# Moving the forget logits into the second half of the values, the spatial weights to another place and other banks, and a layer norm without its centring pass

## The chip, the cores and the metric

The kernel runs on one core of a Trainium2 chip. A core has five engines with queues of their own: TensorE (PE, matrix products into PSUM; PEld is its loading of weights), VectorE (DVE), ScalarE (ACT), GpSimd (POOL), and SyncE (SP), which here only issues DMAs. PSUM has eight banks of 128 x 512 floats. The metric is the device time of one execution in microseconds; the time of a kernel is the median of its runs.

## The reference

One layer of a streaming encoder over 512 positions of width 1024, in float32. What matters for the change is the first projection and the gated branch behind it:

```python
h = rmsnorm(x, norm_mix_g[i])
z = jnp.einsum('bsd,dc->bsc', h, w_in[i])
uv = jax.nn.gelu(z[..., :o1])
z_u, z_v = uv[..., :GMLP_WIDTH], uv[..., GMLP_WIDTH:]
...
v = z[..., o1 + 2 * FOX_WIDTH:o2]
f_logit = z[..., o2:o3]
...
# spatial gating: blocks of 128 positions, 8 groups of 128 channels
v = layernorm(z_v, ln_g, ln_b)
w = jnp.where(mask[None], w_s, jnp.zeros_like(w_s))
mixed = jnp.einsum('gts,bnsgc->bntgc', w, v) + b_s.T[None, None, :, :, None]
return z_u * mixed.reshape(B, S, GMLP_WIDTH)
```

The 16 forget logits of each position go through a log-sigmoid and a running sum over positions, which is added to the attention's scores. Behind the two branches stand the gates, the output projection, a gated MLP with a causal convolution (width 2816), an embedding add and a last RMSNorm.

## The kernel before

Every float32 product is made of three products of a split: a matrix is cut into a high part (a copy rounded to the fast type, on ScalarE, L144, L250 or L366) and a low part (the difference, on VectorE, L145, L251 or L367), and TensorE multiplies low by high, high by low and high by high. One such matmul has 128 x 128 stationary and 512 moving columns. Weights come in 512 KB pieces through a ring of raw buffers ("raw", three, and "more", five) into a ring of five split pairs ("whi", "wlo").

TensorE's order is written out by hand: the blocks with `tc.manual_schedule(engines={ET.PE})` keep the order of the program there. The orders of the other engines are set by a planner when the kernel is built, which simulates the engines and places an instruction when its inputs are due; each engine then works through its fixed order and waits in place.

The stages in question, in TensorE's order:

1. The first half of the values (512 columns, weight rows as moving operand, L227 to L231), woven with the transposes of the normalised input.
2. The forget logits (L554 to L591). Their weights (64 columns, of which 16 count) land in a part of tile S4l, are copied to S2l (L561) and their low part is taken (L562). Sixteen matmuls with 64 output columns (L568) write one bank; then come a chain on ScalarE and VectorE (L571 to L588) and a store to `cum_d`.
3. The second half of the values (`proj_N` with `rb_outer=False`, L612): four weight pairs, and for each the four row blocks, into four banks; 96 matmuls (L153 to L155), with `evac_v` at the end.
4. A gate projection (`gate_steps`, L167 to L171).
5. Two Strassen-like products (`wino_jobs`), for the gelu inputs of v and then of u: seven products P1, P7, P6, P2, P5, P4, P3 of 24 matmuls each, so 336 steps in all. They use as stationary operands the input itself and four sums of its quarters, split in tiles S1 to S4 (sums of L607): S3 serves P7, S2 P6, S1 P5 and S4 P3. Their results stand in banks "sc" (P1 and P2), "pt" (P7 and P4) and "pt", "av" (P6, P5, P3).
6. Inside the second of them stand the layer norm of v (L688 to L703, in tile zv) and the spatial weights: step 168 and 24 more, layer norm, 120 more, the transpose of the bias `bsr` (L708), 12 more, four transposes (L714), 6 more, four transposes, 6 more.
7. Another gate, then eight spatial mixes (`mix`, L719 to L737) woven with gates, and then attention, which reads `cum_d`.

The banks go by tags: "mm" has two, "sc" two, "pt" three, "av" one; an unnamed bank takes the next tag of `BANK_TURN`. The squares of the layer norm, the bias and weight transposes and the gates all use "mm".

Of the kernel before, what the change touches and what calls it, by code (L numbers as in the profile page):

```python
# [9 lines left out]
F32 = mybir.dt.float32  # L10
F32R = mybir.dt.float32r
AF = mybir.ActivationFunctionType
ALU = mybir.AluOpType
PSUM = bass.MemoryType.PSUM

P = 128
S = 512
D = 1024
NB = S // P
NK = D // P  # L20
# [9 lines left out]
N_FIRST = 1  # L30
# [13 lines left out]
def hybrid_block(  # L44
# [6 lines left out]
    nc = tc.nc  # L51
    V, A, G, T = nc.vector, nc.scalar, nc.gpsimd, nc.tensor
# [6 lines left out]
    w_in_v, w_a_v, w_b_v = kview(w_in[0]), kview(w_a[0]), kview(w_b[0])  # L59
# [10 lines left out]
    state = {"n": 0, "bank": 0, "ring": None, "more": None, "raw": 0, "pool": {}, "psum": None}  # L70
# [15 lines left out]
    def bank(tag=None):  # L86
        pool, bufs = state["psum"]
        if tag is None:
            tag = BANK_TURN[state["bank"] % len(BANK_TURN)]
            state["bank"] += 1  # L90
        return pool.tile([P, 512], F32, tag=tag, name=uid("bank"), bufs=bufs[tag])
# [38 lines left out]
    def more_tile():  # L130
        return state["more"].tile([P, D], F32, tag="more", name=uid("more"), bufs=X_BUFS)
# [52 lines left out]
    def load_N(wv, k0, nk, ch, subs=(None, None), between=None):  # L184
        res = []
        for j in range(nk // 2):
            k = k0 + 2 * j
            res.append(load_w(wv[:, k:k + 2, 512 * ch:512 * ch + 512], 2, 512, subs[j % 2]))
            if between:
                between(j)  # L190
        return res

    def proj_N(wv, k0, nk, act, ch, evac, rb_outer=True, subs=None):

        ahi, alo = act
        subs = subs or load_N(wv, k0, nk, ch)

        def part(bk, rb, j):
            r = ds(rb * P, P)
            for kk in range(2):  # L200
                k = 2 * j + kk
                mm3(bk, ahi[:, k, r], alo[:, k, r], subs[j][0][:, kk, :], subs[j][1][:, kk, :],
                    start=(k == 0), stop=(k == nk - 1))
        if rb_outer:
            for rb in range(NB):
                bk = bank()
                for j in range(nk // 2):
                    part(bk, rb, j)
                evac(bk, rb, ch)
        else:  # L210
            bks = [bank() for _ in range(NB)]
            for j in range(nk // 2):
                for rb in range(NB):
                    part(bks[rb], rb, j)
                    if j == nk // 2 - 1:
                        evac(bks[rb], rb, ch)

    def proj_N_steps(wv, k0, nk, act, ch, evac, subs=None):

# [16 lines left out]
    def steps(g, n):  # L236
        for _ in range(n):
            next(g)
# [118 lines left out]
    ident = consts.tile([P, P], F32, tag="ident", name="ident")  # L357
# [102 lines left out]
    def quarter(tag, dt=F32R):  # L460

        return ph.tile([P, D], dt, tag=tag, name=uid(tag))
# [97 lines left out]
    nc.sync.dma_start(wf_raw, w_in_v[:, :, 5120:5184])  # L560
    V.tensor_copy(wf2, wf_raw)  # L561
    V.tensor_tensor(wf2[:, :, 32:48], wf_raw[:, :, 0:16], wf2[:, :, 0:16].bitcast(F32), ALU.subtract)  # L562
    state["bank"] = 3
    bk = bank()
    with tc.manual_schedule(engines={ET.PE}):
        for k in range(8):
            for t in (1, 0):
                T.matmul(bk[0:64, :], wf2[:, k, :], hT[t][:, k, :],  # L568
                         start=(k == 0 and t == 1), stop=(k == 7 and t == 0))
    fz, fa, fb = fm[0][0:16, 0:512], fm[0][0:16, 512:], fm[1][0:16, 0:512]  # L570
    A.copy(fa, bk[32:48, :])  # L571
    V.scalar_tensor_tensor(fz, bk[0:16, :], bft[0:16, :], fa, ALU.add, ALU.add)
# [35 lines left out]
        split_out(sums[(0, 2, 1, 3)[n]], dst, full)  # L608

    state["bank"] = 0  # L610
    with tc.manual_schedule(engines={ET.PE}):
        proj_N(w_in_v[:, :, 4096:5120], 0, NK, hT, 1, evac_v, rb_outer=False)  # L612

    zv = zv_tile().rearrange("p (b c) -> p b c", b=NB)
# [15 lines left out]
    def gate_weights(n):  # L632
        return load_w(w_in_v[:, :, gate_col(n):gate_col(n) + P], 8, P)
# [37 lines left out]
    with tc.manual_schedule(engines={ET.PE}):  # L671
        run(gate_steps(0, "mm", gate_tile, None, G))
        units = wino_steps(wino_jobs(w_in_v, 1024, hT, sums, wino_rows(zv, gelu_zv))
                           + wino_jobs(w_in_v, 0, hT, sums, wino_rows(zu, gelu_zu)))
        steps(units, 168)
        gb = [more_tile(), more_tile()]
        nc.sync.dma_start(gb[0], rows_bc(ln_g[0], D))
        nc.sync.dma_start(gb[1], rows_bc(ln_b[0], D))

        wst = more_tile().rearrange("p (g s) -> p g s", g=8)  # L680
        nc.sync.dma_start(wst, w_s[0].rearrange("g t s -> t g s"))
        G.memset(wst[0:64, :, 64:128], 0.0)
        bsr = ph.tile([P, P], F32, tag="bsr", name="bsr")
        G.memset(bsr, 0.0)
        nc.sync.dma_start(bsr[0:8, :], b_s[0])
        steps(units, 24)

        nm, va = tiny("nm", NB), tiny("va", NB)  # L688
        V.tensor_tensor(nm, zs[:, 0:NB], zs[:, NB:], ALU.add)
        V.tensor_scalar(nm, nm, -1.0 / D, None, ALU.mult)  # L690
        sq = tiny("sq", 2 * NB, 1)
        for rb in range(NB):
            A.activation(zv[:, rb, :], zv[:, rb, :], AF.Identity, bias=nm[:, rb:rb + 1])
            for h in range(2):
                A.activation(bank("mm"), zv[:, rb, 512 * h:512 * h + 512], AF.Square,
                             accum_out=sq[:, NB * h + rb:NB * h + rb + 1])
        V.tensor_tensor(va, sq[:, 0:NB], sq[:, NB:], ALU.add)
        V.tensor_scalar(va, va, 1.0 / D, EPS, ALU.mult, ALU.add)
        y = rsqrt_of(va, NB)
        for rb in range(NB):  # L700
            V.scalar_tensor_tensor(zv[:, rb, :], zv[:, rb, :], y[:, rb:rb + 1], gb[0],
                                   ALU.mult, ALU.mult)
            V.tensor_tensor(zv[:, rb, :], zv[:, rb, :], gb[1], ALU.add)  # L703
        steps(units, 120)

        wsT = [quarter(f"S1{t}").rearrange("p (g t) -> p g t", g=8) for t in "hl"]
        bk = bank("mm")
        T.transpose(bk[:, 0:P], bsr, ident)  # L708
        V.tensor_copy(bsT, bk[:, 0:NK])
        steps(units, 12)  # L710
        for g0 in (0, 4):
            bk = bank("mm")
            for g in range(4):
                T.transpose(bk[:, g * P:(g + 1) * P], wst[:, g0 + g, :], ident)  # L714
            split_out(wsT, bk.rearrange("p (g t) -> p g t", g=4),
                      (slice(None), slice(g0, g0 + 4), slice(None)))
            steps(units, 6)

        def mix(g):  # L719
            c = slice(g * P, g * P + P)  # L720
            vp = quarter(f"S2{'hl'[g % 2]}").rearrange("p (t b c) -> p t b c", t=2, b=NB)
            vh, vl = vp[:, 0], vp[:, 1]
            split_out((vh, vl), zv[:, :, c], (slice(None),) * 3)
            bk = bank("sc")
            mm3(bk, wsT[0][:, g, :], wsT[1][:, g, :], vh, vl, True, True)
            an = quarter(f"S3{'hl'[g % 2]}", F32)[:, 0:512].rearrange("p (b c) -> p b c", b=NB)
            V.scalar_tensor_tensor(an, bk.rearrange("p (b c) -> p b c", b=NB), bsT[:, g:g + 1],
                                   zu[:, :, c], ALU.add, ALU.mult)
            yield
            bk = bank("pt")  # L730
            for n in range(NB):
                T.transpose(bk[:, n * P:(n + 1) * P], an[:, n, :], ident)
            ap = quarter(f"S4{'hl'[g % 2]}").rearrange("p (t r) -> p t r", t=2)
            split_out((ap[:, 0], ap[:, 1]), bk, (slice(None),) * 2)
            for t in range(2):
                G.dma_start(aT_d[t][g * P:g * P + P, :], ap[:, t].bitcast(F32))
            yield  # L737


        first, ahead, w_qk = N_FIRST, [gate_weights(N_FIRST)], []  # L740

        def mix_gates():
            for n in range(first, GATES[0] - 1):
                w = ahead.pop()
                if n + 1 < GATES[0] - 1:
                    ahead.append(gate_weights(n + 1))
                else:

                    w_qk.extend(qk_weights(pr) for pr in range(2))
                yield from gate_steps(n, "mm", gate_tile, w, G)  # L750

        run(units)
        fill = mix_gates()
        steps(fill, 24 * N_COVER)
        ms = [mix(g) for g in range(NK)]
        items = [ms[0], ms[1]]
        for g in range(2, NK):
            items += [ms[g - 2], ms[g]]
        items += [ms[NK - 2], ms[NK - 1]]
        weave(items, fill, 24 * N_MIX)  # L760
        run(fill)
# [234 lines left out]
    bk = bank()  # L996
# [249 lines left out]
```

## Time and profile before

| | us |
|---|---|
| median of 3 runs | 965.3 |
| lowest, highest | 964.53, 966.54 |
| the profiled execution | 964.26 |
| its span, first to last instruction | 962.5 |
| DVE busy | 596.9 |
| ACT busy | 465.6 |
| POOL busy | 118.4 |

The profile shows one execution. A row of a timeline has the start and the duration in us from the span's start, the engine, the line of the kernel, the operation, the tiles written and read, the shape and the count; in brackets stand the idle time of the engine before the row and what ended it. A matmul's displayed duration overlaps with the next one's start, since matmuls are pipelined. "PEclk" is the share of TensorE's full clock that was granted. The mean granted clock of the whole execution is 0.994.

### The profile page before, as it was taken

To read this page: it belongs to the slowest core of one execution; us is meant where nothing else is said; L and a number is where in the kernel's file an instruction comes from. 1 tells how busy PE (TensorE), PEld (TensorE's weight loads), DVE (VectorE), ACT (ScalarE), POOL (GpSimd) and SP (SyncE) were. 2 spreads that over 40 slices of the span, in tenths; PEclk is the share of its full clock that TensorE was granted. 3 is DMA by queue.
4 is the path that set the end of the run, shared out by engine and by line. 5 is a ranking of instruction groups with operands and counts; after the bars stand their busy time and mean duration, and the time that the engine had idled before them with its cause. 6 is when DMAs were issued, how large, how long until landed. Compare 5 with 4: busy or idle time off the path is not lost.

```text
span 962.5 us, 11722 instructions
## 1 busy us (share of the span) xinstructions
PE 936.6 (97%) x4375; PEld 774.9 (81%) x4375; DVE 596.9 (62%) x1025; ACT 465.6 (48%) x779; POOL 118.4 (12%) x116
## 2 busy tenths in 40 slices
PE   8899998999999998999999999999999999999995
PEld 6678886888888887888888888888888888888885
DVE  6866789657777888425644665664356553365754
ACT  7644685466666666424433554443143441244443
POOL 3000000343333201001000400000000000001225
PEclk9999999999999999999999999999999999999998
DMA  9512344753333331199841422224323323223202
GB/s 343 179 59 74 113 142 110 240 164 99 99 99 99 99 99 65 56 328 359 299 157 63 153 88 88 88 88 132 108 73 104 110 88 109 66 88 131 70 18 88
DMA packets 100292, 121.21 MB, mean 126 GB/s; under 512 B 5252, under 2 KB 70972, under 8 KB 100236
## 3 DMA queue, kind: packets, MB, share of 16 engines
q1 hardware_dynamic: 97740, 112.57, 36.1%
q0 software_dynamic: 2352, 7.64, 2.1%
q8 instruction: 34, 0.56, 0.2%
q10 hardware_dynamic: 144, 0.26, 0.1%
q14 instruction: 22, 0.18, 0.1%
HBM read 106.79 MB, written 13.66 MB: 125 GB/s over the span
## 4 chain that ended last, share of the span: by engine, by line
PE 88%; DVE 6%; ACT 2%; issue 1%; DMA 1%; POOL 1%; SPq 0%; POOLq 0%; DVEq 0%
PE bank L167 17%; PE bank L169 17%; PE bank L171 17%; PE bank L153 5%; PE bank L155 5%; PE bank L154 5%; PE bank L227 3%; PE bank L229 3%; PE bank L231 3%; PE bank L306 2%; PE bank L303 2%; PE bank L299 2%; PE bank L861 2%; PE bank L852 1%; PE bank L403 1%
## 5 line engine op out<-in xcount | busy, mean ns | idle before, releaser
L167 PE MATMUL bank<-slot,wlo 128*128 128x512 f32 (+1 forms) x744 | 295.0, 398 | 0.8 <-DVE S1l L367 0.8
L169 PE MATMUL bank<-slot,whi 128*128 128x512 f32 (+1 forms) x744 | 289.0, 389 | 0.0
L171 PE MATMUL bank<-slot,whi 128*128 128x512 f32 (+1 forms) x744 | 288.7, 389 | 0.0
L144 ACT CAST whi<-raw 128x1024 fp32r<-128x1024 f32 x130 | 136.0, 1047 | 137.9 <-PE bank L155 80.1
L145 DVE TENSOR_TENSOR wlo<-raw,whi 128x1024 fp32r<-128x1024 f32 x108 | 132.6, 1229 | 109.2 <-ACT whi L144 108.8
L171 PEld LDWEIGHTS bank<-slot,whi 128*128 128x128 f32 x744 | 139.7, 188 | 29.0
L167 PEld LDWEIGHTS bank<-slot,wlo 128*128 128x128 f32 x744 | 139.9, 188 | 25.0 <-DVE S1l L367 1.3
L169 PEld LDWEIGHTS bank<-slot,whi 128*128 128x128 f32 x744 | 140.2, 188 | 22.5 <-DVE slot L367 0.2
L145 POOL TENSOR_TENSOR wlo<-raw,whi 128x1024 fp32r<-128x1024 f32 x22 | 53.8, 2449 | 518.7 <-ACT whi L144 511.1
L153 PE MATMUL bank<-whi,slot 128*128 128x512 f32 (+1 forms) x232 | 88.6, 382 | 0.0
L155 PE MATMUL bank<-whi,slot 128*128 128x512 f32 (+1 forms) x232 | 88.6, 382 | 0.0
L154 PE MATMUL bank<-wlo,slot 128*128 128x512 f32 (+1 forms) x232 | 88.6, 382 | 0.0
L227 PE MATMUL bank<-whi,slot 128*128 128x512 f32 x152 | 59.9, 395 | 2.6 <-DVE slot L367 2.6
L231 PE MATMUL bank<-whi,slot 128*128 128x512 f32 x152 | 59.6, 392 | 0.0
L229 PE MATMUL bank<-wlo,slot 128*128 128x512 f32 x152 | 59.1, 390 | 0.0
L155 PEld LDWEIGHTS bank<-whi,slot 128*128 128x128 f32 x232 | 43.6, 188 | 8.5
L153 PEld LDWEIGHTS bank<-whi,slot 128*128 128x128 f32 x232 | 43.6, 188 | 8.5
L154 PEld LDWEIGHTS bank<-wlo,slot 128*128 128x128 f32 x232 | 43.6, 188 | 8.4
L1086 DVE SCALAR_TENSOR_TENSOR ul<-bank,cvT,ul 128x511 f32<-128x511 f32 x22 | 16.5, 750 | 50.9 <-ACT ul L1085 50.9
L834 ACT ACTIVATE t<-t,mn 128x512 f32<-128x512 f32 (+1 forms) x64 | 35.9, 562 | 10.4 <-DVE mn L831 7.5
L366 ACT CAST pth<-bank 128x512 fp32r<-128x512 f32 (+1 forms) x64 | 26.3, 428 | 24.8 <-PE bank L852 24.7
L227 PEld LDWEIGHTS bank<-whi,slot 128*128 128x128 f32 x152 | 28.6, 188 | 8.9 <-DVE slot L367 3.4
(278 smaller groups left out, 1357.1 us busy)
## 6 DMA issues: line engine op xcount, KB each, us to landing
raw<-in_w_up_dram SPq DMA_DIRECT2D x44, 512.0 KB, 3.5
raw<-in_w_in_dram SPq DMA_DIRECT2D x36, 512.0 KB, 4.5
raw<-in_w_down_dram SPq DMA_DIRECT2D x22, 512.0 KB, 3.2
more<-in_w_in_dram SPq DMA_DIRECT2D x20, 512.0 KB, 5.3
cum<-cum_d SPq DMA_DIRECT2D x8, 512.0 KB, 4.0
raw<-in_w_branch_b_dram SPq DMA_DIRECT2D x8, 512.0 KB, 3.6
slot<-aT_d SPq DMA_DIRECT2D x4, 1024.0 KB, 12.3
sg<-gate_d SPq DMA_DIRECT2D x16, 256.0 KB, 5.3
```

Source lines behind the costliest of these rows:

```text
L144: A.copy(hi, raw)
L145: (sub or V).tensor_tensor(lo, raw, hi.bitcast(F32), ALU.subtract)
L153: T.matmul(out_ap, alo, bhi, start=start, stop=False)
L154: T.matmul(out_ap, ahi, blo, start=False, stop=False)
L155: T.matmul(out_ap, ahi, bhi, start=False, stop=stop)
L167: T.matmul(out_ap, wl, ah, start=(n == 0 and k == 0), stop=False)
L169: T.matmul(out_ap, wh, al, start=False, stop=False)
L171: T.matmul(out_ap, wh, ah, start=False, stop=end)
L227: T.matmul(bk, alo[:, k, r], wh, start=(k == 0), stop=False)
L229: T.matmul(bk, ahi[:, k, r], wl, start=False, stop=False)
L231: T.matmul(bk, ahi[:, k, r], wh, start=False, stop=(k == nk - 1))
L834: A.activation(t, t, AF.Exp, scale=-1.0, bias=m, accum_out=rs[:, i:i + 1])
```

## The change

It has three parts. The forget logits' sixteen matmuls go from before the second half of the values to behind its first weight pair (24 matmuls), with a hook `after` in `proj_N`; the weights of the values are loaded ahead of them, and the bank counter is set so that the four value banks come first. The spatial weights are loaded into the quarter S3h, at 24 steps behind the layer norm, in place of a "more" buffer; bias and weights are transposed at steps 270, 295 and 301 in "sc" banks, the bias is copied by ScalarE in place of VectorE, and the load of the next gate's weights is issued before the weight transposes. The layer norm no longer centres v in a pass of its own on ScalarE: the squares take the negative mean as a bias, VectorE computes (v - mean) x gain before the variance is known, and then x 1/deviation + offset, where it computed v x 1/deviation x gain and + offset before.

```diff
-    def proj_N(wv, k0, nk, act, ch, evac, rb_outer=True, subs=None):
+    def proj_N(wv, k0, nk, act, ch, evac, rb_outer=True, subs=None, after=None):
...
                     if j == nk // 2 - 1:
                         evac(bks[rb], rb, ch)
+                if after:
+                    after(j)
...
-    state["bank"] = 3
-    bk = bank()
-    with tc.manual_schedule(engines={ET.PE}):
+    state["bank"] = 0
+    subs_v1 = load_N(w_in_v[:, :, 4096:5120], 0, NK, 1)
+    bk_f = []
+
+    def forget(j):
+        if j:
+            return
+        bk_f.append(bank())
         for k in range(8):
             for t in (1, 0):
-                T.matmul(bk[0:64, :], wf2[:, k, :], hT[t][:, k, :],
+                T.matmul(bk_f[0][0:64, :], wf2[:, k, :], hT[t][:, k, :],
                          start=(k == 0 and t == 1), stop=(k == 7 and t == 0))
+
+    with tc.manual_schedule(engines={ET.PE}):
+        proj_N(w_in_v[:, :, 4096:5120], 0, NK, hT, 1, evac_v, rb_outer=False, subs=subs_v1,
+               after=forget)
+    bk = bk_f[0]
...
     state["bank"] = 0
-    with tc.manual_schedule(engines={ET.PE}):
-        proj_N(w_in_v[:, :, 4096:5120], 0, NK, hT, 1, evac_v, rb_outer=False)
...
-        wst = more_tile().rearrange("p (g s) -> p g s", g=8)
-        nc.sync.dma_start(wst, w_s[0].rearrange("g t s -> t g s"))
-        G.memset(wst[0:64, :, 64:128], 0.0)
...
         for rb in range(NB):
-            A.activation(zv[:, rb, :], zv[:, rb, :], AF.Identity, bias=nm[:, rb:rb + 1])
             for h in range(2):
                 A.activation(bank("mm"), zv[:, rb, 512 * h:512 * h + 512], AF.Square,
-                             accum_out=sq[:, NB * h + rb:NB * h + rb + 1])
+                             bias=nm[:, rb:rb + 1], accum_out=sq[:, NB * h + rb:NB * h + rb + 1])
+            V.scalar_tensor_tensor(zv[:, rb, :], zv[:, rb, :], nm[:, rb:rb + 1], gb[0],
+                                   ALU.add, ALU.mult)
...
         for rb in range(NB):
-            V.scalar_tensor_tensor(zv[:, rb, :], zv[:, rb, :], y[:, rb:rb + 1], gb[0],
-                                   ALU.mult, ALU.mult)
-            V.tensor_tensor(zv[:, rb, :], zv[:, rb, :], gb[1], ALU.add)
-        steps(units, 120)
+            V.scalar_tensor_tensor(zv[:, rb, :], zv[:, rb, :], y[:, rb:rb + 1], gb[1],
+                                   ALU.mult, ALU.add)
+        steps(units, 24)
+
+        wst = quarter("S3h", F32).rearrange("p (g s) -> p g s", g=8)
+        nc.sync.dma_start(wst, w_s[0].rearrange("g t s -> t g s"))
+        G.memset(wst[0:64, :, 64:128], 0.0)
+        steps(units, 54)
+        bk = bank("sc")
+        T.transpose(bk[:, 0:P], bsr, ident)
+        A.copy(bsT, bk[:, 0:NK])
+        steps(units, 19)
+
+        first, ahead, w_qk = N_FIRST, [gate_weights(N_FIRST)], []
 
         wsT = [quarter(f"S1{t}").rearrange("p (g t) -> p g t", g=8) for t in "hl"]
-        bk = bank("mm")
-        T.transpose(bk[:, 0:P], bsr, ident)
-        V.tensor_copy(bsT, bk[:, 0:NK])
-        steps(units, 12)
         for g0 in (0, 4):
-            bk = bank("mm")
+            steps(units, 6)
+            bk = bank("sc")
             for g in range(4):
                 T.transpose(bk[:, g * P:(g + 1) * P], wst[:, g0 + g, :], ident)
             split_out(wsT, bk.rearrange("p (g t) -> p g t", g=4),
                       (slice(None), slice(g0, g0 + 4), slice(None)))
-            steps(units, 6)
...
-        first, ahead, w_qk = N_FIRST, [gate_weights(N_FIRST)], []
```

## The prediction

> **What bounds the kernel now.** First the head of the page and its chain that ended last.
>
> ```profile
> span 962.5 us, 11722 instructions
> PE 936.6 (97%) x4375; PEld 774.9 (81%) x4375; DVE 596.9 (62%) x1025; ACT 465.6 (48%) x779; POOL 118.4 (12%) x116
> PE 88%; DVE 6%; ACT 2%; issue 1%; DMA 1%; POOL 1%; SPq 0%; POOLq 0%; DVEq 0%
> ```
>
> TensorE is busy 97% of the span and is 88% of the chain. The change adds and removes no matmul, so only TensorE's gaps and its clock can give time: 962.5 - 936.6 = 25.9 us of gaps. The second view, the waits of TensorE, says which gaps belong to the edited code.
>
> ```profile
> PE bank L568 <- DVE S2l L562: 3.5, 1, 3.5
> PE bank L852 <- DVE ptl L367: 3.2, 3, 1.7
> PE bank L714 <- DVE bsT L709: 2.0, 1, 2.0
> PE bank L167 <- DVE S1l L367: 0.8, 1, 0.8
> ```
>
> The columns after the colon are total, times and longest. Three of these waits lie in the edited stretch: the forget logits (L568) for their split weights, the transposes of the spatial weights (L714) for a copy out of their bank, and the next gate projection (L167) for the bank after that. L852 is in attention, which the change does not touch. Third, the windows around these waits (columns: span, then busy time with count for PE, PEld, DVE, ACT, POOL, then PEclk, DMA share, GB/s).
>
> ```profile
> 46.20:49.00 2.80, 2.80 (x8) 1.54 (x9) 2.80 (x4) 0.00 (x0) 0.00 (x0) 0.61 0.66 192
> 49.00:51.50 2.50, 2.50 (x10) 1.42 (x9) 2.25 (x2) 0.00 (x0) 0.00 (x0) 0.75 0.89 283
> 51.50:154.30 102.80, 102.80 (x456) 84.71 (x454) 78.50 (x94) 59.95 (x88) 1.83 (x3) 1.00 0.32 95
> 124.00:144.00 20.00, 20.00 (x90) 16.54 (x89) 16.45 (x28) 16.88 (x29) 0.52 (x1) 1.00 0.57 165
> 144.00:154.00 10.00, 10.00 (x48) 8.13 (x46) 9.90 (x14) 3.86 (x5) 0.00 (x0) 1.00 0.60 156
> 154.00:164.00 10.00, 7.13 (x33) 5.38 (x32) 10.00 (x14) 6.89 (x10) 0.00 (x0) 1.00 0.35 94
> 159.20:206.00 46.80, 46.79 (x221) 38.67 (x222) 28.80 (x39) 22.60 (x36) 17.79 (x27) 1.00 0.59 192
> ```
>
> Two things are to be seen. After the first gap the granted clock is 0.61 and 0.75 for 5.3 us, so this wait is paid twice. And around the second and third gaps VectorE is full (9.90 of 10, then 10.00 of 10): TensorE waits for work that is small but stands in VectorE's queue. Between and behind the gaps TensorE has no idle time that could be had.
>
> **Part 1: the forget logits go behind the first quarter of the second value half.** The rows of TensorE's order in time (start, duration, line):
>
> ```profile
> 42.23 0.39 PE L231 MATMUL bank<-whi,slot 128*128 128x512 f32 x1
> 46.16 5.47 PE L568 MATMUL bank<-slot,S2l 128*64 128x512 f32 x16 [3.54 <-DVE S2l L562]
> 51.47 0.40 PE L153 MATMUL bank<-whi,slot 128*128 128x512 f32 x1
> ...
> 73.25 0.39 PE L167 MATMUL bank<-slot,wlo 128*128 128x512 f32 x1
> ```
>
> The second value half is 4 weight pairs x 4 row blocks x 6 = 96 matmuls from 51.47 to 73.25: 21.78 / 96 = 0.2269 us from start to start. The displayed 0.39 overlaps with the next one, so I count starts. The first half's last matmul should be followed at 42.23 + 0.23 = 42.46. The forget block starts at 46.16, 3.70 later, and its 16 matmuls take until 51.47, 5.31 us, where 16 x 0.2269 = 3.63 would do at full clock; 64 output columns in place of 128 should not make one longer, and the windows give the clock as the reason. So the place costs 3.70 + 1.68 = **5.38 us**.
>
> Afterwards the values run on at 42.46 if their first weights are split, 24 matmuls cover until 42.46 + 5.45 = 47.91, and then the forget block needs S2l. VectorE's rows:
>
> ```profile
> 41.28 1.22 DVE L145 TENSOR_TENSOR wlo<-more,whi 128x1024 fp32r<-128x1024 f32 x1
> ...
> 45.82 0.28 DVE L562 TENSOR_TENSOR S2l<-S4l,S2l 128x128 fp32r<-128x128 f32 x1
> ...
> 50.03 1.22 DVE L272 TENSOR_TENSOR raw<-more,raw 128x1024 f32<-128x1024 f32 x1
> ```
>
> The first split is done at 42.50, and only the second matmul (at 42.69) reads it: no wait. S2l is done at 46.10, 1.8 us before 47.91. So nothing is left of the stall, and the cover is those 24 matmuls; without them the price is the 3.70 again. Of the moved instructions, the value loads and splits now precede the Strassen sums (L607) in program order, which can only bring them forward in VectorE's queue; the loads on SP have landed by then, as the splits show. The chain behind the logits (log-sigmoid, scan, the store of cum_d) starts when the block ends, 47.91 + 3.63 = 51.54 against 51.47, so it stays put while TensorE moves 5.4 us ahead; its buffers are next read by the third Strassen product, over 30 us later. Cost nothing.
>
> **Part 2: the spatial weights and the bias.** The rows that price it:
>
> ```profile
> 138.53 0.39 PE L299 MATMUL bank<-whi,S1l 128*128 128x512 f32 x1
> ...
> 149.42 0.27 PE L708 MATMUL bank<-ident,bsr 128*128 128x128 f32 x1
> ...
> 153.90 0.40 PE L306 MATMUL bank<-whi,S4h 128*128 128x512 f32 x1
> 156.35 0.66 PE L714 MATMUL bank<-ident,more 128*128 128x128 f32 x4 [2.05 <-DVE bsT L709]
> ...
> 157.99 0.40 PE L306 MATMUL bank<-whi,S4h 128*128 128x512 f32 x1
> 159.21 0.50 PE L167 MATMUL bank<-slot,wlo 128*128 128x512 f32 x1 [0.83 <-DVE S1l L367]
> ...
> 164.83 0.39 PE L153 MATMUL bank<-S2h,S1l 128*128 128x512 f32 x1
> ```
>
> From start to start the stalls are 156.35 - 153.90 - 0.23 = 2.22 and 159.21 - 157.99 - 0.23 = 0.99, together **3.21 us**. The bias transpose moves from step 312 of the 336 (149.42) to step 270, 42 x 0.2269 earlier, at about 139.9; the weights' from 324 and 330 to 295 and 301, about 145.6 and 146.9 (all on the clock of the run before). They use the "sc" banks, which product P2 leaves at 138.53 as the row of P5 shows, so the gate behind them finds its "mm" bank unused and its 0.99 has no cause left. The copy to bsT now goes to ScalarE, which has 124-144 full at 16.88 of 20 but loses 4.3 us there (below), then 3.86 of 10.
>
> What must be ready is wst at step 295. It goes into S3h, dead once P7 is through:
>
> ```profile
> 127.10 0.34 SPq L677 DMA_DIRECT2D more<-in_gmlp_ln_g_dram  x1
> 132.50 0.34 SPq L678 DMA_DIRECT2D more<-in_gmlp_ln_b_dram  x1
> 134.19 0.38 SPq L681 DMA_DIRECT2D more<-in_gmlp_w_s_dram  x1
> ...
> 138.77 0.52 POOL L682 MEMSET more<- 64x512 f32 x1 [58.40 <-issue]
> ```
>
> P7 ends two products of 24 steps before P5 starts at 138.53, so S3h is free at 127.64 and asks for no later issue than 134.19; the clearing on POOL, which waits for the landing, ends at 139.29, 6.3 us before 145.6. On SP the load stands behind the two of the layer norm as before, and the next gate's weights are merely issued earlier, into a buffer that wst no longer takes. Nothing.
>
> **Part 3: layer norm without the centring pass.** By group (last numbers: busy, mean ns):
>
> ```profile
> L695 ACT ACTIVATE bank<-zv 128x512 f32<-128x512 f32 x8 | 4.7, 585 | 0.0
> L693 ACT ACTIVATE zv<-zv,nm 128x1024 f32<-128x1024 f32 x4 | 4.3, 1141 | 0.7 <-DVE nm L690 0.7
> L701 DVE SCALAR_TENSOR_TENSOR zv<-zv,qy,more 128x1024 f32<-128x1024 f32 x4 | 4.9, 1281 | 0.0
> L703 DVE TENSOR_TENSOR zv<-zv,more 128x1024 f32<-128x1024 f32 x4 | 4.8, 1215 | 0.0
> 206.91 0.72 ACT L834 ACTIVATE t<-t,mn 128x512 f32<-128x512 f32 x1
> ```
>
> ScalarE loses 4.3 us. A square with a per-row bias is not in the trace; it lies between the plain one, 0.585, and the exponential with a bias, 0.72, so at most 8 x 0.135 = 1.1 us come back; I take half. It is off TensorE's path. [...] VectorE keeps eight wide passes, four of them 0.07 longer each (+0.26), and loses the 0.15 of L709. But four of the eight move from behind the variance to before it, where VectorE had 20 - 16.45 = 3.55 us free.
>
> **Sum.** 5.38 + 3.21 = 8.59 us. Against the profiled execution's 964.26 (its span 962.5 and 1.76 around it) that gives 955.67; the median of the runs shown is 965.3, 1.04 above the profiled one, so the forecast is **956.7 us**.
>
> **The rivals.** *VectorE's backlog only moves (959.2).* TensorE would reach the first spatial mix (L153, 164.83) 3.21 us earlier against VectorE, at 161.62, and that needs the split of the values:
>
> ```profile
> 132.95 1.21 DVE L251 TENSOR_TENSOR wlo<-more,whi 128x1024 fp32r<-128x1024 f32 x1
> ...
> 163.14 0.68 DVE L367 TENSOR_TENSOR S2h<-zv,S2h 128x512 fp32r<-128x512 f32 x1
> ```
>
> It ended at 163.82. With the same order of work and none of the free 3.55 us used, TensorE waits 163.82 + 0.26 - 161.62 = 2.5 us there; if 2.5 of the 3.55 are filled, nothing. I take nothing, since the last layer norm pass comes before the gates' weight splits that now stand between, so those can step behind. Against it: the gain row is issued only at 127.10, and part of the free time lies before its landing.
>
> *The forget block waits in its new place (962.0).* VectorE is full until about 51.3 (last row of part 1). If L562 is ordered behind all of that, TensorE stands from 47.91 to 51.5 and the clock drops again, so nearly all of the 5.38 is lost and only part 2 remains: 965.3 - 3.2 = 962.1. One wide pass more ahead of it costs nothing, two some 0.5.
>
> *The slow clock is luck (958.4).* If a gap of 3.70 us slows the clock in some executions only, 1.68 of the sum is not there: 965.3 - 6.91. [...] Against it, the other runs (964.53 to 966.54) are none of them 1.68 below the profiled 964.26.
>
> *Slower: VectorE's queue is blocked by the layer norm (968).* The first passes now need the gain row at once, and it was issued at 127.10 and lands some 3.7 us after, the other row after 132.50. Were the order fixed so that both sets of four stand ahead of the Strassen splits, 4.9 us each plus a wait for a landing, the split at 132.95 with its product at 138.53 (4.4 us of slack to its end) is late by about 3 us, the later ones by up to 5, and the mix by the 2.5 above; with another slow clock (1.7) that is 12 us, more than the 8.6 gained. It decides from the point at which over 4.4 us are put ahead of that split.
>
> **How the numbers follow.** Forecast 0.70 (own range 954.5 to 958.0: the spread of the runs and half a us in attention's waits either way), backlog 0.12, forget late 0.07, clock luck 0.05, slower 0.06. The range 954.3 to 961.0 takes in the forecast, the backlog and the clock, and leaves out the forget block's worst and the slower case, some 0.15 with the tails. A measurement can tell about 0.2%, 1.9 us, from no change. Faster by more holds all but the last and half of the worst forget case: 0.90; within 0.04; slower 0.06.
>
> **What would show it.** Right: no wait of the forget matmuls, their 16 in 3.6 us at clock 1.00, the first gate matmul at 67.9 in place of 73.25, no wait in front of transposes or gate 1, the first mix at about 156.2. Wrong: a wait of the forget block or the first mix for VectorE, a Strassen product that waits for wlo, or gaps in attention that were not there.

## The result

The kernel after takes **956.1 us** (median of 4 runs, 955.95 to 956.48) against 965.02 before: a ratio of 0.9909, with a 95% interval of 0.9895 to 0.9923, so 0.9% faster. The forecast was 956.7. The profiled execution took 956.18, its span is 954.4 and its mean clock 0.997, where it was 964.26, 962.5 and 0.994. Taken from the profiled execution alone, the forecast's sum gave 955.67, 0.5 us below the 956.18.

First the waits of TensorE after (total, times, longest). Line numbers have shifted: L575 is now the forget matmul, L727 the weight transposes, L861 attention's transposes (L852 before), L229 the first projection.

```profile
PE bank L861 <- DVE ptl L369: 3.4, 4, 1.7
PE bank L229 <- DVE slot L369: 2.4, 2, 1.2
...
PE bank L154 <- DVE S2h L369: 0.2, 1, 0.2
```

The three waits of the edited stretch are gone from the list. What is new is 0.2 us of the first spatial mix for S2h, and the large ones left are those that stood there before, at the start and in attention. The timeline of TensorE after, at the places of the forecast:

```profile
47.83 3.84 PE L575 MATMUL bank<-slot,S2l 128*64 128x512 f32 x16
...
67.91 0.50 PE L167 MATMUL bank<-slot,wlo 128*128 128x512 f32 x1
...
134.69 0.27 PE L716 MATMUL bank<-ident,bsr 128*128 128x128 f32 x1
...
140.52 0.60 PE L727 MATMUL bank<-ident,S3h 128*128 128x128 f32 x4
142.35 0.60 PE L727 MATMUL bank<-ident,S3h 128*128 128x128 f32 x4
...
156.21 0.39 PE L153 MATMUL bank<-S2h,S1l 128*128 128x512 f32 x1
156.79 0.50 PE L154 MATMUL bank<-S2h,S1h 128*128 128x512 f32 x1 [0.19 <-DVE S2h L369]
```

No row but the last has a bracket. The forget block starts at 47.83 (forecast 47.91), the gate at 67.91 in place of 73.25, the first mix at 156.21 in place of 164.83: 8.62 us earlier, where the forecast's two terms say 8.59. Of these 0.35 go at L154, which starts 0.58 behind L153 and not 0.23.

The block's new place came out a little otherwise than the program writes it. Of the 24 matmuls of the first weight pair, the planner drew seven into the first half of the values (six from 32.73 on and one at 38.31 in TensorE's timeline after), so 17 stand between the end of the first half at 43.97 and the block; the amount of work ahead of the block is the same. The windows over the same stretches (columns as in the prediction: span, PE, PEld, DVE, ACT, POOL, clock, DMA):

```profile
42.50:48.00 5.50, 5.50 (x26) 4.48 (x25) 5.50 (x7) 3.71 (x5) 0.00 (x0) 1.00 0.14 24
48.00:51.50 3.50, 3.50 (x16) 2.06 (x15) 3.50 (x5) 1.05 (x1) 0.00 (x0) 1.00 0.79 244
118.00:138.00 20.00, 20.00 (x90) 16.49 (x89) 19.05 (x24) 14.76 (x27) 0.53 (x1) 1.00 0.57 159
138.00:148.00 10.00, 10.00 (x49) 8.28 (x48) 9.59 (x24) 6.25 (x9) 0.00 (x0) 1.00 1.08 262
148.00:158.00 10.00, 9.81 (x43) 7.79 (x43) 9.36 (x11) 6.07 (x9) 0.54 (x1) 1.00 0.00 1
```

The clock stays at 1.00 through the forget block. In the second Strassen product VectorE fills 19.05 of 20 us (16.45 before, at about the same place of the program), and less is left for later.

### The profile page after: what moved, and what is told of

It reads as the page before. It is cut to its first block, busy times and chain, and to the rows that moved or that the text cites. A ratio compares the mean times of both kernels' runs of the same rounds, so it can differ in the third digit from the quotient of the medians.

```text
span 954.4 us, 11719 instructions
## 1 busy us (share of the span) xinstructions
PE 934.1 (98%) x4375; PEld 773.7 (81%) x4375; DVE 595.4 (62%) x1024; ACT 462.8 (48%) x776; POOL 118.5 (12%) x116
## 4 chain that ended last, share of the span: by engine, by line
PE 90%; DVE 4%; ACT 2%; POOL 1%; issue 1%; DMA 1%; SPq 0%; POOLq 0%; DVEq 0%
PE bank L167 17%; PE bank L169 17%; PE bank L171 17%; PE bank L154 5%; PE bank L155 5%; PE bank L153 5%; PE bank L229 3%; PE bank L233 3%; PE bank L231 3%; PE bank L301 3%; PE bank L305 3%; PE bank L308 3%; PE bank L870 2%; PE bank L861 1%; PE bank L405 1%; PE bank L833 1%
## 5 line engine op out<-in xcount | busy, mean ns | idle before, releaser
L153 PE MATMUL bank<-whi,slot 128*128 128x512 f32 (+1 forms) x232 | 88.7, 382 | 0.0
L154 PE MATMUL bank<-wlo,slot 128*128 128x512 f32 (+1 forms) x232 | 88.5, 382 | 0.0
L229 PE MATMUL bank<-whi,slot 128*128 128x512 f32 x152 | 59.9, 395 | 2.4 <-DVE slot L369 2.4
L153 PEld LDWEIGHTS bank<-whi,slot 128*128 128x128 f32 x232 | 43.6, 188 | 8.5
L154 PEld LDWEIGHTS bank<-wlo,slot 128*128 128x128 f32 x232 | 43.6, 188 | 8.4
L229 PEld LDWEIGHTS bank<-whi,slot 128*128 128x128 f32 x152 | 28.6, 188 | 8.7 <-DVE slot L369 3.3
```

What stands on the lines that cost most here:

```text
L153: T.matmul(out_ap, alo, bhi, start=start, stop=False)
L154: T.matmul(out_ap, ahi, blo, start=False, stop=False)
L229: T.matmul(bk, alo[:, k, r], wh, start=(k == 0), stop=False)
```

## The experiments

Times are medians; "before" is the kernel before on the same chip, 965.25, 964.82 and 965.13 in the three groups. The twelve kernels are listed first, then told one by one.

| kernel | us | ratio to before, 95% interval |
|---|---|---|
| part 1 | 959.67 | 0.9944 [0.9932, 0.9956] |
| part 2 | 967.41 | 1.0024 [1.0015, 1.0034] |
| part 3 | 968.54 | 1.0035 [1.0022, 1.0048] |
| parts 1 and 2 | 962.14 | 0.9971 [0.9962, 0.9980] |
| parts 1 and 3 | 963.25 | 0.9984 [0.9976, 0.9993] |
| parts 2 and 3 | 962.15 | 0.9970 [0.9960, 0.9981] |
| filler | 964.57 | 0.9995 [0.9987, 1.0004] |
| split on GpSimd | 959.44 | 0.9948 [0.9935, 0.9960] |
| bias copy on ScalarE | 965.99 | 1.0011 [1.0002, 1.0019] |
| sc banks, old place | 964.94 | 1.0000 [0.9988, 1.0012] |
| whole, copy on VectorE | 956.08 | 0.9912 [0.9898, 0.9925] |
| whole, mm banks | 956.1 | 0.9912 [0.9898, 0.9925] |

### Part 1 alone

```diff
-    state["bank"] = 3
...
+    with tc.manual_schedule(engines={ET.PE}):
+        proj_N(w_in_v[:, :, 4096:5120], 0, NK, hT, 1, evac_v, rb_outer=False, subs=subs_v1,
+               after=forget)
```

> Part 1 alone (forget logits behind the first weight pair of the second value half), against 965.0 us before. Theory: the place costs the 3.7 us gap and 1.7 us of slow clock, so 959.6 us; the first gate matmul starts at 67.9 in place of 73.25, the sixteen forget matmuls take 3.7 us, and the two later stalls (2.0 and 0.8 us) stay. Rival, the slow clock is luck of an execution: about 961.3. Rival, the gain is given back behind: a larger stall at the weight transposes and 962 or more.

Measured 959.67, 5.6 us below before, and the two later waits stay as they were (2.0 for bsT, 0.8 for S1l). The first term of the sum stands by itself, the clock's share with it: the gap alone would have brought 3.70. The gate started at 69.16 in this profile and not at 67.9: the forget block already starts at 49.13, 1.3 us later than in the whole change's. Shifts from the start of an execution, if smaller ones, are in the profiles of unchanged places too (the forget block at its old place starts at 46.05 to 46.91). From the block to the gate it is 20.0 us here and 20.1 there.

### Part 2 alone, and part 3 alone

```diff
-        wst = more_tile().rearrange("p (g s) -> p g s", g=8)
...
+        wst = quarter("S3h", F32).rearrange("p (g s) -> p g s", g=8)
...
+        bk = bank("sc")
         T.transpose(bk[:, 0:P], bsr, ident)
-        V.tensor_copy(bsT, bk[:, 0:NK])
+        A.copy(bsT, bk[:, 0:NK])
```

> Part 2 alone (spatial weights in S3h, transposes at steps 270, 295, 301 in sc banks, copy to bsT on ScalarE; the layer norm keeps its centring pass). Theory, place and banks caused both stalls: they go and 961.8 us. Rival, VectorE's backlog is what sets the end here and the stall only moves to the first spatial mix (up to 2.5 us there): 964.3 us.

Measured 967.41: **slower**, outside both expectations. The two waits went and a larger one came. TensorE's timeline in this run:

```profile
165.08 0.79 PE L153 MATMUL bank<-S2h,S1l 128*128 128x512 f32 x1 [2.14 <-ACT S2h L366]
...
167.45 0.79 PE L154 MATMUL bank<-S2h,S1h 128*128 128x512 f32 x1 [1.58 <-DVE S2h L367]
```

and VectorE's queue in front of them:

```profile
160.98 1.22 DVE L700 TENSOR_TENSOR zv<-zv,more 128x1024 f32<-128x1024 f32 x1
162.12 1.21 DVE L145 TENSOR_TENSOR wlo<-more,whi 128x1024 fp32r<-128x1024 f32 x1
163.25 1.28 DVE L352 TENSOR_TENSOR slot<-bank,slot 128x512 f32<-128x512 f32 x2
164.45 1.21 DVE L145 TENSOR_TENSOR wlo<-more,whi 128x1024 fp32r<-128x1024 f32 x1
165.58 1.21 DVE L145 TENSOR_TENSOR wlo<-raw,whi 128x1024 fp32r<-128x1024 f32 x1
166.72 0.68 DVE L367 TENSOR_TENSOR S2h<-zv,S2h 128x512 fp32r<-128x512 f32 x1
```

and ScalarE's:

```profile
162.98 0.59 ACT L644 COPY gt<-bank 128x512 f32<-128x512 f32 x1 [3.29 <-PE bank L171]
163.46 1.05 ACT L144 CAST whi<-raw 128x1024 fp32r<-128x1024 f32 x1
164.41 0.62 ACT L366 CAST S2h<-zv 128x512 fp32r<-128x512 f32 x1
```

The last offset pass (L700) ends at 162.20, but ScalarE's half of the split (L366) starts only at 164.41. In ScalarE's fixed order the read-out of the gate's bank (L644) and a weight split for later stand ahead of it, and the read-out waits, with ScalarE idle for 3.29 us, until TensorE is through with the gate. This order is what the first wait (2.14 us of TensorE) is for. VectorE's own half stands behind three more weight splits for later projections (1.58 us). TensorE comes to the mix sooner, the two halves of the split do not. The windows behind it show the clock:

```profile
165.00:170.00 5.00, 3.34 (x7) 2.35 (x8) 4.22 (x6) 2.21 (x5) 0.00 (x0) 0.50 0.50 151
170.00:175.00 5.00, 5.00 (x21) 4.00 (x21) 2.17 (x4) 1.21 (x2) 0.54 (x1) 0.82 0.02 4
```

So the new wait is paid twice as well: 3.7 us of gap, and a clock of 0.50 and 0.82 for the ten us behind its start.

```diff
-            A.activation(zv[:, rb, :], zv[:, rb, :], AF.Identity, bias=nm[:, rb:rb + 1])
...
+                             bias=nm[:, rb:rb + 1], accum_out=sq[:, NB * h + rb:NB * h + rb + 1])
+            V.scalar_tensor_tensor(zv[:, rb, :], zv[:, rb, :], nm[:, rb:rb + 1], gb[0],
+                                   ALU.add, ALU.mult)
```

> Part 3 alone (layer norm without the centring pass; weights and banks as before). If VectorE's full queue caused the stalls of part 2's place, its relief is enough without new banks: the waits for bsT and S1l go and about 962 us. If place and banks caused them, the copy to bsT still stands behind wide passes: 964.5 to 965 us.

Measured 968.54: slower again, by more, and outside both expectations. The bsT wait is gone, but in its place stands one of the gate for the bank of the weight transposes (TensorE's timeline, then VectorE's):

```profile
161.81 0.80 PE L167 MATMUL bank<-slot,wlo 128*128 128x512 f32 x1 [5.20 <-DVE S1l L367]
```

```profile
151.26 1.23 DVE L145 TENSOR_TENSOR wlo<-more,whi 128x1024 fp32r<-128x1024 f32 x1 [3.19 <-ACT whi L144]
...
153.01 0.15 DVE L391 TENSOR_TENSOR qt<-qy,qh 128x4 f32<-128x4 f32 x1
...
153.68 0.15 DVE L709 COPY bsT<-bank 128x8 f32<-128x8 f32 x1
...
155.15 4.87 DVE L702 SCALAR_TENSOR_TENSOR zv<-zv,qy,more 128x1024 f32<-128x1024 f32 x4
159.94 1.22 DVE L145 TENSOR_TENSOR wlo<-more,whi 128x1024 fp32r<-128x1024 f32 x1
161.07 0.68 DVE L367 TENSOR_TENSOR S1l<-bank,S1h 128x512 fp32r<-128x512 f32 x1
```

The transposes of the old place (L714, at 152.8 and 154.6) now come just ahead of the four offset passes as the planner laid them, and their read-out stands behind 4.87 us of them. The passes themselves come late: VectorE stood idle for 3.19 us for ScalarE's half of a weight split (first row), with the last steps of 1/deviation, which the passes need, queued behind it (L391, the second row, is the first of them). The same idle time is in the profile of parts 1 and 3 (3.10 us) and is only 0.3 us in those of parts 2 and 3 and of the kernel after. In the old place the spatial weights hold a "more" buffer, of which these weights need one too; no run shows whether that delays their load. Behind the wait of 5.20 us the granted clock is 0.50 between 160 and 165 us and 0.85 in the next five.

### Pairs

The edits are those of the parts above, two at a time.

> Parts 1 and 2 without part 3, against 956.1 us of the whole change. If part 3 earns nothing by itself: 956.1. If it is what keeps VectorE in time for the first mix: a wait of the first mix for S2h of 1 to 2.5 us and 957.1 to 958.6 us. The fixed order of the queues could also make it slower than that if the offset pass is placed ahead of splits.

Measured 962.14, 6.0 us above the whole change and above both priced expectations. Same picture as part 2: waits of 2.1 and 1.9 us of the first mix, with the gate's read-out ahead of ScalarE's half, then a clock of 0.50 between 160 and 165 us. Part 3 is worth these 6.0 us where part 2 stands, though alone it costs 3.3. TensorE's waits in this run:

```profile
PE bank L153 <- ACT S2h L368: 2.1, 1, 2.1
PE bank L154 <- DVE S2h L369: 1.9, 1, 1.9
```

> Parts 1 and 3 without part 2 (spatial weights in a more buffer, transposes at steps 312 to 336 in mm banks, copy to bsT on VectorE). Theory, part 2 is worth its 3.2 us on top of the others: 959.3 us with both stalls there. Rival, the relief of VectorE by part 3 removes the stalls already: 956.1 to 957 us.

Measured 963.25, with a wait of 5.9 us of the gate for S1l. Neither expectation; part 2 is worth 7.2 us where part 3 stands, more than the 3.2 of its term, and much of it again behind the long wait's slow clock (0.63 and 0.69 between 155 and 165 us).

> Parts 2 and 3 without part 1. Alone part 2 was 0.2% and part 3 0.4% slower than before, the one for a wait at the first mix, the other for a wait of the gate on S1l. Theory, each takes away the other's new wait: both stalls gone, the forget gap of 3.5 us stays, 965.0 - 3.2 = 961.8 us. Rival, their losses add and it is part 1 that makes room: 968 us or more.

Measured 962.15, 3.0 us below before, as the theory says: the waits of the layer norm's stretch are gone but for the 0.2 at the mix. So parts 2 and 3 are one term, and parts 1 and 2+3 add: 5.6 + 3.0 = 8.6, where the whole change measured 8.9.

### Why the forget logits waited

```diff
+        for _ in range(16):
+            T.matmul(bk, hT[0][:, 0, 0:P], hT[0][:, 0, :], start=True, stop=True)
         for k in range(8):
```

> The kernel before with sixteen extra full-width matmuls, whose product nobody reads, in front of the forget matmuls at their old place. They take 16 x 0.227 = 3.6 us and fill the gap of 3.7 us, so the forget block starts as late as before. Theory, the idle gap slows the clock: the granted clock stays at 1.00, the forget block takes 3.6 in place of 5.3 us, and the time is 965.0 - 1.7 = 963.3 us. Rival, the slowness is the block's own (64 columns, its operands): its matmuls stay at 0.33 us apart and 965.0 us.

Measured 964.57, inconclusive as an experiment on the gap: the planner keeps the order within such a block, but it drew eight of the extra matmuls into the first half and 17 of the values ahead of the forget block, after which the values waited 1.2 us for the forget block's bank. That wait takes up most of the 1.7 us of clock that were to be gained. One thing can be read from it. With no gap ahead, the sixteen took

```profile
49.62 3.84 PE L570 MATMUL bank<-slot,S2l 128*64 128x512 f32 x16
```

as in the kernel after; so the 5.47 before were the clock's and not the 64 columns'.

```diff
-    V.tensor_tensor(wf2[:, :, 32:48], wf_raw[:, :, 0:16], wf2[:, :, 0:16].bitcast(F32), ALU.subtract)
+    G.tensor_tensor(wf2[:, :, 32:48], wf_raw[:, :, 0:16], wf2[:, :, 0:16].bitcast(F32), ALU.subtract)
```

> The kernel before with one engine changed: the low part of the forget weights (L562) on GpSimd, which is idle there, in place of VectorE. Place of the forget logits as before. Theory, the gap of 3.5 us is only that small operation's place in VectorE's queue: the copy before it is done at 41.4, so the weights are ready at about 42 and the forget matmuls start at 42.5 at full clock, 959.7 us as with part 1 alone. Rival, the wait passes to the first weights of the values or to the copy itself: 962 to 965 us.

Measured 959.44, what part 1 brings (959.67), with the forget logits at their old place. GpSimd's and TensorE's rows:

```profile
41.67 1.37 POOL L562 TENSOR_TENSOR S2l<-S4l,S2l 128x128 fp32r<-128x128 f32 x1 [18.19 <-DVE S2l L561]
```

```profile
43.10 3.90 PE L568 MATMUL bank<-slot,S2l 128*64 128x512 f32 x16 [0.26 <-POOL S2l L562]
```

GpSimd needs 1.37 us where VectorE needed 0.28, and yet the operands are there 3 us sooner, because nothing stands ahead of it. The gap of 3.5 us was the place of one small instruction in VectorE's queue.

### Engine and banks of the weight transposes

```diff
-        V.tensor_copy(bsT, bk[:, 0:NK])
+        A.copy(bsT, bk[:, 0:NK])
```

> The kernel before with one line changed: the copy to bsT on ScalarE in place of VectorE. Theory, the second set of transposes waits for that copy only because it stands in VectorE's queue: the 2.2 us go, the 0.99 us of the gate stays or grows a little since the split of the bank behind it is still VectorE's: 962.8 to 963.5 us. Rival, the wait passes to the next use of VectorE (the split of the first four transposes): 965.0 us.

This edit is made in the kernel before. Measured 965.99, slightly slower than before: the 2.0 us for bsT are gone, but the wait passed to the next use of VectorE, 3.0 us of the gate for S1l, which was 0.8. The rival's mechanism holds; its time, 965.0, is 1.0 us short, and in the profile the clock behind the longer wait is 0.69 between 160 and 165 us, where it was 1.00 before.

```diff
-        bk = bank("mm")
+        bk = bank("sc")
         T.transpose(bk[:, 0:P], bsr, ident)
...
-            bk = bank("mm")
+            bk = bank("sc")
             for g in range(4):
```

> The kernel before with the transposes of bias and spatial weights in sc banks, at their old place, copy to bsT on VectorE. The second set still needs the bank of the bias and waits for VectorE's copy; the gate behind finds its mm bank free. Theory: the wait of 2.2 us stays, that of 0.99 goes: 964.0 us. Rival, the banks alone are the cause: 961.8 us.

This edit is made in the kernel before. Measured 964.94: of the waits, bsT's 2.1 us stay and S1l's is gone, but no time is gained on the interval; in its profile the clock is lower (0.991 against 0.994), the forget block took 6.38 us, and the first mix starts at 166.06 against 164.83.

That S1l's wait is gone does not show the work of the banks. Behind the wait for bsT the clock fell in this profile (0.73 between 155 and 160 us), so that TensorE came to the gate later. The same is in two profiles that leave these banks as before, the filler's and that of the split on GpSimd. TensorE's timeline and a window of the filler (the bsT wait, then the clock in the last column but two):

```profile
155.81 0.97 PE L716 MATMUL bank<-ident,more 128*128 128x128 f32 x4 [2.07 <-DVE bsT L711]
155.00:160.00 5.00, 4.19 (x14) 3.49 (x15) 5.00 (x8) 4.47 (x8) 0.00 (x0) 0.66 0.36 101
```

There too the gate does not wait for S1l, and from the first weight transposes to the first mix it is 13.0 us in all three profiles, against 12.52 before. Banks alone do nothing that can be measured.

```diff
-        A.copy(bsT, bk[:, 0:NK])
+        V.tensor_copy(bsT, bk[:, 0:NK])
```

> The whole change with the copy to bsT on VectorE in place of ScalarE. Its bank is needed again 31 steps (7 us) later by the second set of weight transposes. Theory, VectorE's queue delays the copy by less than that: 956.1 us, the engine does not matter. Rival, the copy comes too late again: a wait of the transposes of 1 to 2 us, 957 to 958.5 us.

This edit is made in the kernel after. Measured 956.08. The copy (L717) now waits in VectorE's queue until 136.05, and its bank is needed again only by the second set, at about 142. The engine does not matter.

```diff
-        bk = bank("sc")
+        bk = bank("mm")
         T.transpose(bk[:, 0:P], bsr, ident)
...
-            bk = bank("sc")
+            bk = bank("mm")
             for g in range(4):
```

> The whole change with the transposes of bias and weights in mm banks at their new place. The gate comes 35 steps (8 us) after the second set and needs an mm bank that the first set filled. Theory, the place is what counts, the bank is read out long before the gate: 956.1 us. Rival, the bank counts: the gate waits for S1l as it did with parts 1 and 3, 957 us or more.

This edit is made in the kernel after. Measured 956.1, with the same list of waits. Nor do the banks matter at the new place. Neither of the two beats the kernel after beyond its interval.

## Why the prediction was right, and where its steps were not

**What bounds.** Right. TensorE's gaps in the edited stretch and the clock behind one of them were what could be had, and they were had: the span fell by 8.1 us and TensorE's start of the first mix by 8.6. One reading was too favourable: part 2's price has nothing for the clock behind the gap of 2.22 us in front of the weight transposes. That holds for the profiles before (1.00 from 154 to 164 us) and of part 1 (matmuls 0.23 us from start to start behind it), but in three others the clock behind it fell to between 0.66 and 0.73 over five us (sc banks at the old place, filler, split on GpSimd). It cost little there, 0.5 us up to the mix, since the wait for S1l fell away in return.

**Part 1, 5.38 us.** Right in size (5.6 alone) and in the moments, with one row misread. The split at 41.28 that I took for the first pair of the second value half is the second pair's; the first had been split long before (VectorE's timeline before, a row that the prediction did not show):

```profile
25.39 1.23 DVE L145 TENSOR_TENSOR wlo<-more,whi 128x1024 fp32r<-128x1024 f32 x1 [0.32 <-ACT whi L144]
```

The conclusion (no wait where the values run on) held the better for it. S2l was not done at 46.10 again but at 42.70, and the second pair's split moved behind it, to 46.1 from 42.5, 5.4 us before the second quarter that needs it (VectorE's timeline after):

```profile
42.42 0.28 DVE L564 TENSOR_TENSOR S2l<-S4l,S2l 128x128 fp32r<-128x128 f32 x1
...
44.90 1.22 DVE L145 TENSOR_TENSOR wlo<-more,whi 128x1024 fp32r<-128x1024 f32 x1
```

The new cover of 24 matmuls was therefore larger than this order of VectorE needed, and the split on GpSimd shows that it was not the only cure. Part 1 thus did two things at once: TensorE came to the block later, and the planner laid the small operation earlier.

**Part 2, 3.21 us.** The size is right where part 3 stands with it (3.0 us for the two), the reason is wrong in two details. I gave the gain to the banks ("the gate behind them finds its mm bank unused") and to the copy on ScalarE. With either put back the time is the same. What is left of part 2 is the new place, the buffer S3h and the earlier issue of the gate's weights, which no run takes apart. The profile after speaks for the place: the splits of the transposes (S1l, at 141.78 and 144.66) stand ahead of the offset passes (147.81) in VectorE's queue and are done well ahead of the gate.

**Part 3, "off TensorE's path".** Wrong as a statement, though the sum came out. I priced it at nothing and took part 2's term as its own. Alone, part 2 is 2.2 us slower than before and part 3 3.3 us; together they are 3.0 faster. The step that failed is the one that adds edits to the same queue as if each stood alone. What part 3 does is what the first rival describes: it takes a set of four wide passes out of VectorE's most crowded stretch. How much of its worth is these passes, and how much the other order in which the planner then laid VectorE's and ScalarE's queues, the runs do not separate.

The ScalarE side was mis-sized a little. The squares with a bias took (by group, after)

```profile
L699 ACT ACTIVATE bank<-zv,nm 128x512 f32<-128x512 f32 x8 | 5.4, 680 | 0.6 <-DVE nm L695 0.6
```

0.680 us against 0.585 without (L695 before), +0.095 each and 0.76 in all; I took 0.55.

**The rival of the backlog.** Its mechanism is real and its price was too low. I put 2.5 us on it from the old order of work. Without part 3 it costs 6.0, because on ScalarE the planner laid the gate's read-out ahead of the mix's split, because on VectorE it laid weight splits for later projections there, and because the clock drops behind the wait (to 0.50 between 160 and 165 us in parts 1 and 2). In the kernel after, ScalarE's half starts at 152.71, as soon as the offset passes are done and ahead of the gate's read-out. My reason for giving the backlog nothing, that those splits would step behind the mix, is not what happened: after, two of them still stand in between (VectorE's timeline after),

```profile
147.81 4.87 DVE L707 SCALAR_TENSOR_TENSOR zv<-zv,qy,more 128x1024 f32<-128x1024 f32 x4
152.59 1.22 DVE L145 TENSOR_TENSOR wlo<-more,whi 128x1024 fp32r<-128x1024 f32 x1
153.73 1.28 DVE L354 TENSOR_TENSOR slot<-bank,slot 128x512 f32<-128x512 f32 x2
154.93 1.21 DVE L145 TENSOR_TENSOR wlo<-more,whi 128x1024 fp32r<-128x1024 f32 x1
156.06 0.68 DVE L369 TENSOR_TENSOR S2h<-zv,S2h 128x512 fp32r<-128x512 f32 x1
```

and the mix waits 0.19 us. The passes were early enough by about nothing; had the planner put one more split there, the kernel after would be about 1.2 us slower (an estimate from the duration of such a row).

**The rival of the clock.** I argued from three runs that the slow clock comes every time. More runs of the kernel before, 35 in one group, went from 962.27 to 966.49, and the lowest four (962.27 to 962.48) have a mean clock of 0.997, while those above 966 have 0.991. The same forget block behind the same gap of 3.5 us took 5.47 us in the profile before, 5.46 in part 3's, and in part 2's (timeline of TensorE)

```profile
46.42 6.62 PE L568 MATMUL bank<-slot,S2l 128*64 128x512 f32 x16 [3.55 <-DVE S2l L562]
```

So what the clock costs does vary from one execution to the next, as the rival had it. But the rival's time did not come. Part 1 alone brought 5.6 us, 1.9 more than its gap, and its interval (4.2 to 6.6) leaves the gap's 3.70 out, so the clock's share is in the median. Of the 35 runs, 29 lie at least 1.68 us above the mean of the lowest four; that these four lost nothing to the clock is an assumption, since none of them was profiled. The kernel after spreads over 0.5 us in its four runs, but its variants with the copy on VectorE and with mm banks, whose waits are the same, over 1.8 and 1.6, so the smaller spread is not shown to be the clock's.

**The blocked queue.** The first gain passes did stand for a landing, 0.7 us of VectorE (L701 for the gain row), and no Strassen product waited. The forget block did not wait in its new place.

## What to carry to other kernels

When TensorE waits for something small, look at what stands ahead of it in the queue of the engine that makes it: moving TensorE's use, or the small operation to an idle engine, gave 5.6 and 5.7 us here. Edits that lean on the same crowded queue cannot be priced one by one: two that each lost 0.2 to 0.4% alone gained 0.3% together, so a split of a change into parts should try pairs too. And look at every queue that makes the operand: in part 2 alone the first wait was for ScalarE's fixed order, not for VectorE's. Lastly, a wait can be paid twice, in the gap and in the clock behind it: here waits of 2.05 to 5.9 us had a clock of 0.50 to 0.73 over five us behind them, and others of 2.05 us (before, part 1) had 1.00.

## What the runs showed of the hardware

The price of the clock behind a gap is not fixed: the sixteen forget matmuls, which take 3.84 us at full clock (after, filler), took 5.46 (part 3) to 6.62 us (part 2) behind gaps of 3.5 us. A gap of 2.05 us in front of the weight transposes left the clock at 1.00 in the profiles before and of part 1, where the matmuls behind it stand 0.23 us from start to start; one of 2.05 to 2.07 us at the same place was followed by a mean clock of 0.73, 0.66 and 0.70 over five us in those of the sc banks at the old place, the filler and the split on GpSimd, with matmuls 0.42 to 0.43 us from start to start. A 128 x 128 subtraction, in pieces of 16 columns, took GpSimd 1.37 us and VectorE 0.28.
